# One level of Strassen for the up projection of a ConvFFN, with a separate down projection and buffers placed by lifetimes

## The chip, the cores and the metric

The kernel runs on one core of a Trainium2 chip. A core has TensorE (matrix products into PSUM, "PE" in the profile; its weight loads are "PEld"), VectorE ("DVE"), ScalarE ("ACT"), GpSimd ("POOL") and SyncE ("SP"), whose queue issues all of this kernel's DMAs. The metric is the device time of one execution in microseconds, as the median of several runs.

## The reference, cut to what matters

One layer (`DEPTH = 1`) of a backbone over 2048 latent tokens and 128 context tokens, `D_MODEL = 1024`, `D_FF = 2816`, all in float32: adaLN-modulated norm, a bidirectional HGRN2 mixer with eight heads, gated residual; then adaLN-modulated norm, a ConvFFN, gated residual; final norm.

```python
def conv_ffn(h, w_up, conv_w, conv_b, w_down, grid_axis):
    a, g = jnp.split(h @ w_up, 2, axis=-1)
    a = token_conv(a, conv_w, conv_b, grid_axis)
    return (jax.nn.silu(a) * g) @ w_down
...
hp = modulate(xp, norm_ffn_w[l], mod_p[3], mod_p[4])
hs = modulate(xs, norm_ffn_w[l], mod_s[3], mod_s[4])
xp = xp + mod_p[5] * conv_ffn(hp, ffn_w_up[l], ffn_conv_w[l], ffn_conv_b[l], ffn_w_down[l], None)
xs = xs + mod_s[5] * conv_ffn(hs, ffn_w_up[l], ffn_conv_w[l], ffn_conv_b[l], ffn_w_down[l], 2)
y_prompt = rms_norm(xp, final_norm_w)
y_sample = rms_norm(xs, final_norm_w)
```

`token_conv` is a convolution of width 3 along the tokens of a grid row (64 tokens) for the latent tokens, along the whole sequence for the context.

## The kernel before

Features lie on partitions, tokens along the free axis. The 2176 tokens are five pieces: four of 512 latent tokens (p = 0 to 3) and the context with 128 (`CTX`, p = 4). Each float32 product is made of three float16 products (`mm3`, L301 to L304): both factors are split into a high and a low float16 part, and high x high, high x low and low x high add up in PSUM. All matmuls of the projections are recorded under L302, L303 and L304, so a profile tells them apart by their tiles.

The stages follow each other: adaLN and norm 1 (0 to about 60 us), eight heads of HGRN2 (each has projections for all pieces, between which the scan's small products are set), the output projection with norm 2 (`project`, L841; `norm2`, L867), and the ConvFFN from about 1395 us on.

The ConvFFN runs eleven rounds `c2`, each over two blocks of 128 channels of the 22. A round loads six weight tiles (`ffn_weights`, L880: a and g of the up projection for two blocks, and two blocks of w_down), which `load_w` (L291) casts to a high part on ACT (L296) and a low part on DVE (L299). For each piece and block, `up` (L940) makes 24 products for a and 24 for g, 512 columns wide, with eight blocks of K; then the convolution on ACT and DVE (L952 to L958), SiLU (L960), the product with g (L961) and the split of u (L963, L964). `down` (L967) of the piece before comes between the two blocks' `up`: eight output blocks m, each six products over the round's two blocks of u, which DVE adds to the residual in SBUF (L974). The last round splits piece 3 into two halves of 256 tokens and starts the final norms (`final_norm`, L921) between its pieces; L931 (DVE) and L933/L934 (ACT and POOL) scale the outputs in turn.

A norm is a generator: `begin` runs its first step (squares on ACT, L246 and L249, sums on DVE, L250), and each later `tick` one more: the sum over features on TensorE (L254), the power on POOL (L230), a diagonal (L232), its spread over the partitions on TensorE (L240), and the modulation (`modulated`, L272: L277 and L286 on DVE, L281 on ACT).

SBUF tiles come from one pool in which every tag has a number of slots (`BUFS`, L81): eight of 4 KB for weights (`wp`), two for their raw form (`wr`), 32 for `H`, which hold first the normed inputs and later the residuals. A tile waits for the release of its slot. PSUM has two tags of four banks each: `pj` for projections, `sc` for the rest. The waits between engines are put in by the framework. The instructions of one engine are not strictly in the order of the text: on ACT, the weight casts of the next round (L296) run between steps of `up` (L952, L960) that the text has earlier.

## Time and profile before

| what | value |
|---|---|
| median of 3 runs | 2891.61 us (2889.58 to 2893.44) |
| span of the profiled execution | 2890.3 us |
| TensorE busy | 2847.3 us, 99% of the span |
| VectorE busy | 1747.1 us, 60% |
| ScalarE busy | 830.9 us, 29% |
| mean granted TensorE clock | 0.995 |
| one round of the ConvFFN | 132.7 us |

Of the profiled execution the profile gives the span, from its first to its last instruction; the three times are of other executions. A busy TensorE says little alone: its products overlap in the records (a product of 512 columns is recorded with 0.38 us, while the next starts 0.22 us after it), so the distance of the starts is what counts. A row of a group of instructions reads: line, engine, operation, output <- inputs, shapes, count, then the busy time in us and the mean ns of one, then the idle time before them and what ended it.

### The profile page before, as it was taken

To read this page: it belongs to the slowest core of one execution; us is meant where nothing else is said; L and a number is where in the kernel's file an instruction comes from. 1 tells how busy PE (TensorE), PEld (TensorE's weight loads), DVE (VectorE), ACT (ScalarE), POOL (GpSimd) and SP (SyncE) were. 2 spreads that over 40 slices of the span, in tenths; PEclk is the share of its full clock that TensorE was granted. 3 is DMA by queue.
4 is the path that set the end of the run, shared out by engine and by line. 5 is a ranking of instruction groups with operands and counts; after the bars stand their busy time and mean duration, and the time that the engine had idled before them with its cause. 6 is when DMAs were issued, how large, how long until landed. Compare 5 with 4: busy or idle time off the path is not lost.

```text
span 2890.3 us, 46289 instructions
## 1 busy us (share of the span) xinstructions
PE 2847.3 (99%) x18968; PEld 1675.7 (58%) x18968; DVE 1747.1 (60%) x4854; ACT 830.9 (29%) x1761; POOL 91.9 (3%) x101
## 2 busy tenths in 40 slices
PE   8999999999999999999999999999999999999996
PEld 4677777777777777655544445454545444454555
DVE  7978787878776767757564444343434444443457
ACT  5533333333433333324231112121212111111233
POOL 0100000000000000000000000000000000000013
PEclk9999999999999999999999999999999999999998
DMA  7011202020201020431101000010101010010002
GB/s 275 19 61 33 83 30 86 28 88 28 88 11 47 11 63 17 169 106 31 43 7 38 16 29 30 15 44 1 44 1 44 2 43 15 30 30 15 15 30 95
DMA packets 60867, 134.67 MB, mean 47 GB/s; under 512 B 8560, under 2 KB 18928, under 8 KB 60656
## 3 DMA queue, kind: packets, MB, share of 16 engines
q1 hardware_dynamic: 60656, 131.73, 14.1%
q8 instruction: 148, 2.42, 0.3%
q14 instruction: 63, 0.52, 0.1%
HBM read 112.83 MB, written 18.87 MB: 46 GB/s over the span
## 4 chain that ended last, share of the span: by engine, by line
PE 84%; DVE 10%; issue 1%; ACT 1%; DMA 1%; POOL 1%; POOLq 0%; DVEq 0%; ACTq 0%
PE pj L304 18%; PE pj L303 18%; PE pj L302 18%; PE sc L302 5%; PE sc L304 5%; PE sc L303 5%; PE pj L426 3%; PE pj L425 3%; PE pj L424 3%; PE sc L578 2%; PE sc L538 1%; PE sc L547 1%; DVE og L212 1%; PE sc L616 1%; PE sc L613 1%
## 5 line engine op out<-in xcount | busy, mean ns | idle before, releaser
L304 PEld LDWEIGHTS <-wp 128*128 128x128 f16 x3968 | 388.6, 98 | 368.0 <-issue 3.7
L302 PEld LDWEIGHTS <-wp 128*128 128x128 f16 x3968 | 389.7, 98 | 358.1 <-issue 5.6
L303 PEld LDWEIGHTS <-wp 128*128 128x128 f16 x3968 | 388.9, 98 | 358.8 <-issue 7.5
L974 DVE SCALAR_TENSOR_TENSOR H<-sc,g,H 128x512 f32<-128x512 f32 (+1 forms) x360 | 263.8, 738 | 137.3 <-PE sc L304 137.3
L302 PE MATMUL pj<-H,wp 128*128 128x512 f16 x880 | 334.7, 381 | 3.3 <-ACT H L281 3.3
L303 PE MATMUL pj<-H,wp 128*128 128x512 f16 x880 | 334.9, 381 | 0.8 <-DVE H L286 0.6
L304 PE MATMUL pj<-H,wp 128*128 128x512 f16 x880 | 335.4, 381 | 0.0
L956 DVE SCALAR_TENSOR_TENSOR SB<-pj,cws,SB 128x504 f32<-128x504 f32 (+2 forms) x112 | 73.4, 655 | 349.5 <-ACT SB L952 349.5
L952 ACT ACTIVATE SB<-pj,pv,cws 128x512 f32<-128x512 f32 (+2 forms) x112 | 79.2, 707 | 703.1 <-PE pj L304 702.0
L425 PE MATMUL pj<-wp,H 128*128 128x256 f16 x1024 | 279.4, 273 | 0.6 <-DVE wp L299 0.6
L426 PE MATMUL pj<-wp,H 128*128 128x256 f16 x1024 | 279.4, 273 | 0.0
L424 PE MATMUL pj<-wp,H 128*128 128x256 f16 x1024 | 279.4, 273 | 0.0
L961 DVE SCALAR_TENSOR_TENSOR SB<-pj,SB 128x512 f32<-128x512 f32 (+2 forms) x112 | 67.5, 602 | 246.3 <-PE pj L304 243.7
L299 DVE SCALAR_TENSOR_TENSOR wp<-wr,wp 128x1024 f16<-128x1024 f32 x106 | 128.8, 1224 | 88.1 <-ACT wp L296 76.1
L296 ACT ACTIVATE wp<-wr 128x1024 f16<-128x1024 f32 x106 | 110.1, 1049 | 118.3 <-DMA wr<-w_in 74.1
L960 ACT ACTIVATE SB<-SB 128x512 f32<-128x512 f32 (+2 forms) x112 | 62.6, 559 | 162.7 <-DVE SB L958 162.6
L426 PEld LDWEIGHTS <-H 128*128 128x128 f16 x1024 | 100.2, 98 | 12.4 <-issue 0.7
L425 PEld LDWEIGHTS <-H 128*128 128x128 f16 x1024 | 100.2, 98 | 11.7
L424 PEld LDWEIGHTS <-H 128*128 128x128 f16 x1024 | 100.2, 98 | 11.3
L397 ACT ACTIVATE f<-pj 128x512 f32<-128x512 f32 x64 | 38.0, 596 | 174.7 <-PE pj L304 174.4
L304 PE MATMUL pj<-op,wp 128*128 128x512 f16 (+1 forms) x232 | 87.2, 376 | 0.0
L303 PE MATMUL pj<-op,wp 128*128 128x512 f16 (+1 forms) x232 | 87.2, 376 | 0.0
(357 smaller groups left out, 5928.0 us busy)
## 6 DMA issues: line engine op xcount, KB each, us to landing
wr<-w_up SPq DMA_DIRECT2D x44, 512.0 KB, 4.0
wr<-w_in SPq DMA_DIRECT2D x40, 512.0 KB, 4.0
wr<-adaT SPq DMA_DIRECT2D x32, 512.0 KB, 3.6
wr<-w_down SPq DMA_DIRECT2D x22, 512.0 KB, 3.8
sp<-oT SPq DMA_DIRECT2D x32, 256.0 KB, 2.4
H<-xT SPq DMA_DIRECT2D x32, 256.0 KB, 4.6
yT<-H SPq DMA_DIRECT2D x24, 256.0 KB, 2.2
wr<-w_out SPq DMA_DIRECT2D x8, 512.0 KB, 4.2
```

The lines of the kernel that those rows point to most:

```text
L296: A.activation(dsthi, r3, AF.Copy, scale=scale)
L299: V.scalar_tensor_tensor(dstlo, r3, scale, dsthi, ALU.mult, ALU.subtract)
L302: T.matmul(out, whl[0], hhl[:, 0, :n], start=first, stop=False)
L303: T.matmul(out, whl[0], hhl[:, 1, :n], start=False, stop=False)
L304: T.matmul(out, whl[1], hhl[:, 0, :n], start=False, stop=last)
L424: T.matmul(o, hp[k][:, 0, tok], wvg[0][:, k], start=(k == 0), stop=False)
L425: T.matmul(o, hp[k][:, 0, tok], wvg[1][:, k], start=False, stop=False)
L426: T.matmul(o, hp[k][:, 1, tok], wvg[0][:, k], start=False, stop=(k == KT - 1))
L952: A.activation(y[:, :n], pa[:, :n], AF.Identity, bias=cbias, scale=w1)
L956: V.scalar_tensor_tensor(y3[:, :, 1:], a3[:, :, : row - 1], w0, y3[:, :, 1:], ALU.mult, ALU.add)
L961: V.scalar_tensor_tensor(y[:, :n], pg[:, :n], IWS, y[:, :n], ALU.mult, ALU.mult)
L974: V.scalar_tensor_tensor(x, pd[:, :n], g64[:, 1, m, s : s + 1], x, ALU.mult, ALU.add)
```

## The change

The kernel's text is built twice: once against stand-ins that count operations and note each tile's first and last use, then, with the addresses that `place` finds from these lifetimes, for the chip. There are no more slots: each tile has an address of its own for its lifetime, and what it must wait for is what used that address before. Tiles older than AGE operations take the first address that is free; younger ones the address that has been and stays free the longest. HGRN2 and what lies before it keep their operations.

The up projection takes blocks of two channel blocks (256 channels) by 1024 features by 512 tokens, and halves each of the three: w_up into A11 to A22, the normed input into B11 to B22. Seven products (`PROD`) of four K blocks and 256 columns take the place of eight, in the order 1, 2, 6, 5, 7, 3, 4, for a and g in turn. Three PSUM banks (A, B, C) hold running sums, which are read between products: each copy (ACT) and each addition (DVE) takes 256 columns into the four quarters c11 to c22 of an output tile in SBUF. `quad` makes the seven weight operands (A11, A12, A21, A22, S1 to S4) for a or g, each split in two parts; `operands` makes the seven input operands once for each piece, after the norm, in the place of the residual, which `keep` has written to DRAM before. The context's up projection keeps its products, with the weights A11 to A22.

After the products, `gate` does the convolution, SiLU and the product with g from SBUF; u is written to DRAM (`put_u`). Steps of `quad`, `gate` and `load_wd` wait in a list, `pending`, from which `post` takes one after each pair of products. When all 22 blocks are done, `down` runs over the pieces: for each of eight output blocks 66 products over all 22 channel blocks into one bank, one addition to the residual (read back from DRAM), and a final norm for each piece, with DVE alone scaling the outputs. w_down is loaded by output block (eight tiles of 22 blocks), during the last round of the up projection; u is read in 14 and 8 blocks for each piece.

```diff
--- before.py
+++ after.py
+def place(tiles, FAR, AGE):
+    at = [0] * len(tiles)
+    for grain, lo, hi, some in (
+            (TINY, 0, TINIES, [i for i, t in enumerate(tiles) if t.size <= 256]),
+            (GRAIN, TINIES, ARENA, [i for i, t in enumerate(tiles) if t.size > 256])):
+        slots = (hi - lo) // grain
+        lives = [[] for _ in range(slots)]
+        size = lambda i: -(-tiles[i].size // grain)
+        age = lambda i: tiles[i].last - tiles[i].born
+        some.sort(key=lambda i: (-age(i) // AGE if age(i) > AGE else 0, -min(size(i), 16),
+                                 tiles[i].born))
+        for i in some:
+            t, n = tiles[i], size(i)
+            packed = age(i) > AGE
+            room = []
+            for s in range(slots):
+                lv = lives[s]
+                j = bisect.bisect(lv, (t.born, 0))
+                before = t.born - lv[j - 1][1] + 1 if j else NEVER
+                after = lv[j][0] - t.last + 1 if j < len(lv) else NEVER
+                room.append(min(before, after))
+            step = 1 if n < 2 else 2 if n < 3 else 4
+            best, where = 0, -1
+            for st in (step, 1):
+                for s in range(0, slots - n + 1, st):
+                    g = min(FAR, *room[s : s + n])
+                    if g > best:
+                        best, where = NEVER if packed else g, s
+                if where >= 0:
+                    break
+            if where < 0:
+                return None
+            for s in range(where, where + n):
+                bisect.insort(lives[s], (t.born, t.last))
+            at[i] = lo + where * grain
+    return at
...
+    def keep(p):
+        n = PIECES[p][1]
+        xsp[p] = drt([P, KT, n], F32, f"xsp{p}")
+        for i in range(0, KT, 2):
+            nc.sync.dma_start(xsp[p][:, i : i + 2], X[p][:, i : i + 2])
+    def split(dst, src, scale=None):
+        A.activation(dst[0], src, AF.Copy)
+        V.tensor_tensor(dst[1], src, dst[0], ALU.subtract)
+    def operands(p, x):
+        TT[p] = {}
+        def half2(z, src):
+            t = TT[p][z] = tl([P, 2, 4, HN], F16, "T")
+            split((t[:, 0], t[:, 1]), src)
+        b11, b12, b21, b22 = (x[:, 4 * k : 4 * k + 4, HN * j : HN * j + HN]
+                              for k in range(2) for j in range(2))
+        half2("B11", b11)
+        half2("B21", b21)
+        yield
+        half2("B22", b22)
+        V.tensor_tensor(b11, b12, b11, ALU.subtract)
+        half2("T1", b11)
+        yield
+        V.tensor_tensor(b12, b22, b12, ALU.subtract)
+        half2("T3", b12)
+        V.tensor_tensor(b22, b22, b11, ALU.subtract)
+        half2("T2", b22)
+        yield
+        V.tensor_tensor(b21, b21, b22, ALU.subtract)
+        half2("T4", b21)
+    def norm2(p):
+        x = X[p]
+        n = PIECES[p][1]
+        s = int(p == CTX)
+        keep(p)
+        def finish(bc):
+            for k in range(KT):
+                V.scalar_tensor_tensor(x[:, k], x[:, k], wmod[:, 1, k, s : s + 1], bc[:, :n],
+                                       ALU.mult, ALU.mult)
+                A.activation(x[:, k], x[:, k], AF.Identity, bias=mod[:, 24 + k, s : s + 1])
+                if k == 3:
+                    yield
+            yield
+            if p == CTX:
+                TT[p] = tl([P, 2, KT, n], F16, "T")
+                split((TT[p][:, 0], TT[p][:, 1]), x)
+            else:
+                yield from operands(p, x)
+        def steps():
+            bc = []
+            yield from norm([x[:, k] for k in range(KT)], n, ["s", "s", "s"], "s", V, bc.append)
+            yield from finish(bc[0])
+        begin(steps())
...
+    def quad(cb, i):
+        w = {}
+        WQ[cb, i] = w
+        def part(z, src):
+            t = w[z] = tl([P, 2, 512], F16, "w7")
+            A.activation(t[:, 0], src, AF.Copy, scale=WS)
+            V.scalar_tensor_tensor(t[:, 1], src, WS, t[:, 0], ALU.mult, ALU.subtract)
+        raw = []
+        for j in range(2):
+            raw.append(tl([P, D], F32, "r"))
+            nc.sync.dma_start(raw[j], w_up[cb + j, i])
+        yield
+        a11, a12, a21, a22 = (raw[j][:, 512 * k : 512 * k + 512]
+                              for j in range(2) for k in range(2))
+        part("A11", a11)
+        part("A12", a12)
+        yield
+        s1, s2 = tl([P, 512], F32, "s"), tl([P, 512], F32, "s")
+        V.tensor_tensor(s1, a21, a22, ALU.add)
+        V.tensor_tensor(s2, s1, a11, ALU.subtract)
+        part("S2", s2)
+        yield
+        part("S1", s1)
+        s3 = tl([P, 512], F32, "s")
+        V.tensor_tensor(s3, a11, a21, ALU.subtract)
+        part("S3", s3)
+        yield
+        s4 = tl([P, 512], F32, "s")
+        V.tensor_tensor(s4, a12, s2, ALU.subtract)
+        part("S4", s4)
+        part("A22", a22)
+        part("A21", a21)
+    WQ = {}
+    PROD = {1: ("A11", "B11", "A", True), 2: ("A12", "B21", "B", True),
+            6: ("S2", "T2", "A", False), 5: ("S1", "T1", "C", True),
+            7: ("S3", "T3", "A", False), 3: ("S4", "B22", "C", False),
+            4: ("A22", "T4", "A", False)}
+    def product(q, i, w, T7):
+        za, zb, bank, first = PROD[i]
+        if first:
+            q[bank] = pt([P, 512], "pj" if bank == "A" else "sc")
+        out = q[bank][:, :HN]
+        wt, tt = w[za], T7[zb]
+        for k in range(4):
+            ks = slice(k * P, k * P + P)
+            for n, (a, b) in enumerate(((0, 0), (0, 1), (1, 0))):
+                T.matmul(out, wt[:, a, ks], tt[:, b, k], start=first and k == 0 and n == 0,
+                         stop=i in (2, 3, 4) and k == 3 and n == 2, skip_group_check=True)
+        sc = q["scale"]
+        (c11, c12), (c21, c22) = ([m[:, HN * j : HN * j + HN] for j in range(2)] for m in q["out"])
+        def add(dst, src):
+            V.scalar_tensor_tensor(dst, src, sc, dst, ALU.mult, ALU.add)
+        if i == 1:
+            A.activation(c11, out, AF.Copy, scale=sc)
+        elif i == 2:
+            add(c11, out)
+        elif i == 6:
+            A.activation(c12, out, AF.Copy, scale=sc)
+        elif i == 7:
+            A.activation(c22, out, AF.Copy, scale=sc)
+            add(c22, q["C"][:, :HN])
+        elif i == 3:
+            add(c12, out)
+        elif i == 4:
+            A.activation(c21, out, AF.Copy, scale=sc)
...
+    def put_u(y, cb, p, n):
+        u = tl([P, 2, 512], F16, "u")
+        split((u[:, 0, :n], u[:, 1, :n]), y[:, :n])
+        USP[cb, p] = drt([P, 2, n], F16, f"u{cb}_{p}")
+        nc.sync.dma_start(USP[cb, p], u[:, :, :n])
+    pending = []
+    def post(n=1):
+        for _ in range(n):
+            while pending and next(pending[0], 0) == 0:
+                pending.pop(0)
+    def gate(cb, p, qa, qg):
+        for j in range(2):
+            y = conv(qa["out"][j], cb + j, p, 512)
+            yield
+            V.tensor_tensor(y, y, qg["out"][j], ALU.mult)
+            put_u(y, cb + j, p, 512)
+            yield
+    def up(cb, p):
+        qa, qg = ({"scale": s, "out": [tl([P, 512], F32, "c7") for _ in range(2)]}
+                  for s in (1.0, IWS))
+        for i in (1, 2, 6, 5, 7, 3, 4):
+            product(qa, i, WQ[cb, 0], TT[p])
+            product(qg, i, WQ[cb, 1], TT[p])
+            post()
+            tick()
+        pending.append(gate(cb, p, qa, qg))
+    def up_ctx(cb):
+        n = NCTX
+        for j in range(2):
+            pa, pg = pt([P, 512], "pj"), pt([P, 512], "pj")
+            for pp, i in ((pa, 0), (pg, 1)):
+                for k in range(KT):
+                    wt = WQ[cb, i][("A11", "A12", "A21", "A22")[2 * j + k // 4]]
+                    ks = slice(k % 4 * P, k % 4 * P + P)
+                    mm3(pp[:, :n], (wt[:, 0, ks], wt[:, 1, ks]), TT[CTX][:, :, k], n,
+                        k == 0, k == KT - 1)
+            y = conv(pa[:, :n], cb + j, CTX, n)
+            V.scalar_tensor_tensor(y[:, :n], pg[:, :n], IWS, y[:, :n], ALU.mult, ALU.mult)
+            put_u(y, cb + j, CTX, n)
+            post()
+    WD = {}
+    U = {}
...
+    def load_wd(m):
+        w = tl([P, 2, NCB, P], F16, "wd")
+        WD[m] = w
+        for c0, c1 in ((0, 11), (11, 22)):
+            raw = tl([P, 11, P], F32, "rawd")
+            nc.sync.dma_start(raw, w_down[c0:c1, :, m * P : (m + 1) * P]
+                              .rearrange("k p c -> p k c"))
+            A.activation(w[:, 0, c0:c1], raw, AF.Copy, scale=WS)
+            V.scalar_tensor_tensor(w[:, 1, c0:c1], raw, WS, w[:, 0, c0:c1],
+                                   ALU.mult, ALU.subtract)
+            yield
+    def load_u(p, cbs):
+        n = PIECES[p][1]
+        for cb in cbs:
+            u = tl([P, 2, n], F16, "U")
+            nc.sync.dma_start(u, USP[cb, p])
+            U[p, cb] = u
+    XD = {}
+    def down(p, m, c, n):
+        s = int(p == CTX)
+        x = tl([P, n], F32, "x")
+        nc.sync.dma_start(x, xsp[p][:, m, c : c + n])
+        pd = pt([P, 512], "pj")
+        for cb in range(NCB):
+            mm3(pd[:, :n], (WD[m][:, 0, cb], WD[m][:, 1, cb]), U[p, cb][:, :, c : c + n], n,
+                cb == 0, cb == NCB - 1)
+        V.scalar_tensor_tensor(x, pd[:, :n], g64[:, 1, m, s : s + 1], x, ALU.mult, ALU.add)
+        XD.setdefault((p, c), []).append(x)
...
+    pending.extend([quad(0, 0), quad(0, 1)])
     for m in range(KT):
         project(3, ALL, (m,))
         project(CTX, ALL, (m,))
         tick()
         if m == 1:
             norm2(2)
+        if m > 1:
+            post(2)
+    post(20)
+    norm2(3)
+    norm2(CTX)
+    for cb in range(0, NCB, 2):
+        last = cb + 2 == NCB
+        for p in range(CTX):
+            up(cb, p)
+            if p == 1 and cb:
+                up_ctx(cb)
+            if not last and p in (1, 2):
+                pending.append(quad(cb + 2, p - 1))
+            if last:
+                pending.extend([load_wd(2 * p), load_wd(2 * p + 1)])
+                if p == 2:
+                    load_u(0, range(14))
+        if cb == 0:
+            up_ctx(cb)
+    post(100)
+    load_u(0, range(14, NCB))
+    for p in range(CTX + 1):
+        n = PIECES[p][1]
+        for m in range(KT):
+            down(p, m, 0, n)
+            tick()
+            if m == 3 and p < CTX:
+                load_u(p + 1, range(14))
+        if p < CTX:
+            load_u(p + 1, range(14, NCB))
+        final_norm(p, 0, n, [V])
     while norms:
         tick()
```

364 lines of the change are left out of this document (159 added, 205 removed), and 5 rows, old and new, of the table BUFS.

## The prediction

> **What bounds the kernel now.** I read the page first, then the shapes on TensorE, then tables by stage.
>
> ```profile
> span 2890.3 us, 46289 instructions
> PE 2847.3 (99%) x18968; PEld 1675.7 (58%) x18968; DVE 1747.1 (60%) x4854; ACT 830.9 (29%) x1761; POOL 91.9 (3%) x101
> PE 84%; DVE 10%; issue 1%; ACT 1%; DMA 1%; POOL 1%; POOLq 0%; DVEq 0%; ACTq 0%
> ...
> 434.70:579.50 144.80, 144.14 (x1209) 104.02 (x1207) 116.97 (x449) 51.71 (x137) 5.28 (x5) 1.00 0.19 58
> 868.50:1012.50 144.00, 144.00 (x1209) 103.97 (x1207) 98.96 (x417) 51.90 (x137) 5.06 (x5) 1.00 0.09 29
> ...
> 1296.00:1399.00 103.00, 102.10 (x638) 54.92 (x637) 73.75 (x113) 38.74 (x55) 3.03 (x3) 1.00 0.16 49
> 1399.00:1477.00 78.00, 78.00 (x372) 36.61 (x371) 46.24 (x73) 23.09 (x39) 1.55 (x2) 1.00 0.02 7
> 1531.70:1664.40 132.70, 132.54 (x722) 64.43 (x721) 57.51 (x86) 24.07 (x37) 0.00 (x0) 1.00 0.08 24
> ```
>
> The last rows are stages (start:end, length, then busy time of PE, PEld, DVE, ACT, POOL; granted clock; DMA share; GB/s): two heads of HGRN2, the output projection, the first 78 us of the ConvFFN, one ConvFFN round of two channel blocks. TensorE is busy without a hole in each, at a granted clock of 1.00. Busy time alone doesn't prove saturation, since products overlap; the starts do:
>
> ```profile
> 1899.69 0.38 PE L303 MATMUL pj<-V,wp 128*128 128x512 f16 x1
> ...
> 1908.54 0.22 PE L302 MATMUL pj<-q,wp 128*128 128x128 f16 x1
> ...
> 2808.75 0.27 PE L302 MATMUL pj<-k,wp 128*128 128x256 f16 x1
> ...
> 2813.99 0.38 PE L302 MATMUL sc<-o,wp 128*128 128x512 f16 x1
> ...
> 1911.22 0.38 PE L302 MATMUL sc<-o,wp 128*128 128x512 f16 x1
> ...
> L304 PEld LDWEIGHTS <-wp 128*128 128x128 f16 x3968 | 388.6, 98 | 368.0 <-issue 3.7
> ```
>
> From 1899.69 to 1908.54 start 41 products of 512 columns: 0.2159 us each. From there to 1911.22 start 48 of 128 columns: 0.0558 each. From 2808.75 to 2813.99 start 48 of 256 columns (the last round halves piece 3): 0.1092 each. So columns set the time, and a 256-column product costs 0.506 of a 512-column one, its weight load (98 ns in the last row) hidden. A round holds 4 x 144 products of 512 and 144 of 128: 124.4 + 8.0 = 132.4 us, against 132.7 in the row. The stage is saturated: only less TensorE work, or idle time outside it, can shorten the kernel.
>
> **The change, term by term.**
>
> *Up products.* Before, a round takes 4 pieces x 96 products of 512 columns; over 11 rounds 4224 x 0.2159 = 912.0 us. After, each piece takes 7 block products x 12 x 2 (a and g) = 168 of 256 columns: 7392 x 0.1092 = 807.2 us. **Saved: 104.8 us.** Context up products and all down products keep their numbers and widths (528 x 4 of 512 columns); down only sums over 22 blocks in PSUM instead of 2.
>
> The Trainium skill, "TensorE: Matmul & The Clock Gate", section "Back-to-back issue gap", also gives a gap of N/2.4 + 2.5 ns; it says too that a stream of load and product pairs holds about 81 ns at N=128 and 131 ns at N=512. By the second rule the new products would cost at least 7392 x 81 ns = 599 us against 553 us before, a loss; the trace (55.8 and 215.9 ns) contradicts it.
>
> *Vector and scalar work beside the up products.*
>
> ```profile
> L974 DVE SCALAR_TENSOR_TENSOR H<-sc,g,H 128x512 f32<-128x512 f32 x344 | 256.4, 750 | 137.3 <-PE sc L304 137.3
> L974 DVE SCALAR_TENSOR_TENSOR H<-sc,g,H 128x256 f32<-128x256 f32 x16 | 7.4, 478 | 0.0
> L956 DVE SCALAR_TENSOR_TENSOR SB<-pj,cws,SB 128x504 f32<-128x504 f32 x86 | 63.9, 743 | 338.1 <-ACT SB L952 338.1
> L964 DVE TENSOR_TENSOR og<-SB,og 128x512 f16<-128x512 f32 x22 | 15.2, 692 | 13.6 <-ACT og L963 13.6
> L299 DVE SCALAR_TENSOR_TENSOR wp<-wr,wp 128x1024 f16<-128x1024 f32 x106 | 128.8, 1224 | 88.1 <-ACT wp L296 76.1 <-PE pj L304 11.2
> L952 ACT ACTIVATE SB<-pj,pv,cws 128x512 f32<-128x512 f32 x86 | 66.9, 778 | 601.3 <-PE pj L304 600.2 <-DVE og L250 0.6 <-DVE Am L286 0.5
> L960 ACT ACTIVATE SB<-SB 128x512 f32<-128x512 f32 x86 | 54.1, 630 | 142.7 <-DVE SB L958 142.7
> L618 ACT ACTIVATE op<-sc 128x256 f32<-128x256 f32 x64 | 23.8, 372 | 19.1 <-PE sc L616 19.1
> ```
>
> Columns: busy us, mean ns of one, then idle before. Per piece: six Strassen additions out of PSUM at 0.48 = 2.9 us on DVE and eight copies at 0.37 = 3.0 on ACT; the gate twice, each (2 x 0.743 + 2 x 0.692) = 2.9 on DVE and (0.778 + 2 x 0.63) = 2.0 on ACT. Per round two `quad`s, each seven parts at 0.75 plus four sums at 0.69 = 8.0 us DVE and seven casts at 0.63 = 4.4 ACT. A round: DVE 4 x 8.7 + 16 + 2.5 (context) = 53 us, ACT 4 x 7 + 8.8 + 2.2 = 39, against 4 x 168 x 0.1092 + 5.4 = 78.8 us of TensorE. Both fit under it. What is new is a tight hand-off: bank C is read (ACT copy of product 7, then DVE addition) before product 3 may write it. From the last start of 7a: 0.27 + 0.37 + 0.48 us plus hand-overs is about 1.2; TensorE has the 12 products of 7g in between, 13 x 0.1092 = 1.4 us. It just fits if both engines are free. The two HGRN2 rows show what crowded engines cost: DVE at 117 instead of 99 us of 144 cost 0.8 us, 0.6%. Bounds: 0 (hidden) to 12 us a round (the slower rival). I take 1.4 us a round, near that row with a little for the round's edge, where `quad` of g comes late: **+15 us.** A wait there holds the products behind it, and nothing else.
>
> *The entry of the ConvFFN.* Norm 2 of a piece had 16 DVE operations of 0.75 (12 us); now it has 8, seven splits and four differences of 1024 elements. The nearest rows give 1.22 to 2 x 0.69, so 6 + 11 x 1.33 = 20.6: 8.7 us more. The 1296:1399 row leaves 29 us free on DVE; three norms add about 24 and quads instead of six weight casts (7.3) add 8.7, so DVE is over full, 4 us behind. Then piece 3 needs its norm (7 additions, 20.6: 26 us), the context 6, four pieces' additions 12 and three gates 17, together 61, within the 55 us of three pieces that hide it, 10 us behind; a second round of quads, 16, follows in the same queue. **+18 us**, bounds 0 (gates put off) and 35 (all overhang paid, chain latency too).
>
> *Tail.*
>
> ```profile
> 2826.00:2866.00 40.00, 35.51 (x367) 31.41 (x365) 33.93 (x62) 16.84 (x42) 14.34 (x10) 1.00 0.28 106
> 2866.00:2891.00 25.00, 7.04 (x48) 5.92 (x47) 14.99 (x37) 3.61 (x12) 7.74 (x10) 0.55 0.32 105
> ...
> 2870.03 1.01 PE L254 MATMUL pj<-ones,kvb 128*128 128x1 f32 x4 [3.19 <-DVE kvb L250]
> 2880.86 0.28 DVE L250 TENSOR_TENSOR kvb<-kvb,qb 128x128 f32<-128x128 f32 x1
> ```
>
> TensorE's last product ends 3.2 us before 2870.03, at 2866.8; the last norms still run then, and 4.5 of the 40 us before are idle. After, norms of pieces 0 to 2 lie beside the next piece's 114 us of down products, that of piece 3 beside the context's 29 us, and only the context's is left: from the last sum (2880.86) to the end 9.4 us, plus about 1.1 for the last update and square. 23.5 - 10.5 + 4.5, about **-18 us**, bounds -22 and -8.
>
> *Turn from up to down.* Before it is nothing: both alternate. Now 8 weight blocks (11.5 MB) and piece 0's u (5.8 MB) have to be there.
>
> ```profile
> 1180.00:1200.00 20.00, 19.41 (x207) 15.70 (x204) 7.95 (x20) 8.51 (x18) 0.00 (x0) 1.00 0.94 341
> wr<-w_down SPq DMA_DIRECT2D x22, 512.0 KB, 3.8
> ```
>
> 17.3 MB at 341 GB/s are 51 us, inside the last round's 79. Their SP issues share the queue with 10 stores of u; a load queued behind the last gate's store waits for it. The first 14 blocks of u are 42 products, 9 us of cover. **+5 us**, bounds 0 and 30. Storing u (24.5 MB) and reading it again, and x, is hidden at a DMA share of 0.08.
>
> *Buffers.*
>
> ```profile
> 22.37 1.06 ACT L296 ACTIVATE wp<-wr 128x1024 f16<-128x1024 f32 x1 [3.99 <-DMA wr<-w_in]
> ```
>
> HGRN2 at 144 us a head is at its products' floor, so there is little to gain; at the start weights come late through the two slots of `wr` (4 us here). **-2 us**, bounds -8 and +8 (an address reused too soon makes a DMA wait, and SP's queue behind it).
>
> Sum: 2890.3 - 104.8 + 15 + 18 - 18 + 5 - 2 = 2803.5. Medians stand 1.3 us above this span (2891.6 against 2890.3): **2805 us**.
>
> **Rivals.**
>
> *All hidden* (20%). DVE's 53 of 79 us leaves room; entry, hand-offs and turn at nothing or nearly (4 us): 2891.6 - 104.8 - 18 - 8 + 4 = 2765. Against it: DVE's overhang at the entry is counted work.
>
> *DVE and ACT become the bound of the up stage: slower* (12%). A gate's half is one chain over both: 0.78 + 1.49 + 0.63 + 0.69 + 0.63 + 0.69 = 4.9 us. Were both queues bound to the program's order, nothing would run beside it, and a piece with a quad beside it would take 9.8 + 5.9 (copies, additions) + 8.6 = 24.3 us instead of 18.3; two such pieces a round lose 12 us, 132 in all: 2805 - 15 + 132 = 2922. It decides from a loss of 9 us a round on. Against it:
>
> ```profile
> 1910.09 0.46 ACT L952 ACTIVATE SB<-pj,pv,cws 128x128 f32<-128x128 f32 x1
> 1910.44 1.04 ACT L296 ACTIVATE wp<-wr 128x1024 f16<-128x1024 f32 x1
> 1911.64 0.31 ACT L960 ACTIVATE SB<-SB 128x128 f32<-128x128 f32 x1 [0.15 <-DVE SB L958]
> ```
>
> The weights of the next round (L296), written later in the program, run between two steps of one context block (L952, L960): the queues are filled by readiness.
>
> *Addresses and DMAs* (14%). w_down now comes in 512-byte pieces, and long-lived tiles take the first address free, even one just read. If the turn costs 30 us and each of four later pieces 2: 2805 - 5 + 38 = 2838.
>
> *Narrow products cost more than half* (1%). A weight load of 98 ns that isn't hidden would make 7392 x 0.207 = 1530 us of the up products, and 3510 in all; the 48 starts above speak against it. The second rule of the Trainium skill's page above is of this kind, milder: 46 us lost by its figures.
>
> **How the numbers follow.** Forecast 2805 has 53%. The range, 2762 to 2860, takes in the hidden case and the addresses, and leaves out the slower rival and some of its milder forms. A measurement here tells about 0.2% (6 us) from no change. Faster: forecast, hidden and addresses less small tails, 0.84; within 0.2%: 0.03; slower: 0.13.
>
> **What would show it.** Right: TensorE starts at 0.109 us throughout up; a round of up near 80 us; holes in TensorE in 1300 to 1480 released by DVE; one short norm behind the last product. Wrong: holes before product 3 or 7 in every round released by ACT or DVE (slower rival); at the turn, TensorE released by DMAs of u or w_down (addresses); heads longer than 144.8 us.

## The result, and the profile after

| | before | after |
|---|---|---|
| median of 4 runs | 2892.23 us (2889.58 to 2893.44) | 2792.88 us (2789.91 to 2796.14) |
| ratio | | 0.9656, 95% interval 0.9642 to 0.967 |
| span of the profiled execution | 2890.3 us | 2788.1 us |

The change makes the kernel 3.4% faster, 102.2 us by the two spans. The first lines and the chain of the page of the changed kernel:

```profile
span 2788.1 us, 53502 instructions
PE 2745.6 (98%) x21992; PEld 1974.3 (71%) x21992; DVE 1709.5 (61%) x4924; ACT 1007.6 (36%) x2233; POOL 68.3 (2%) x80
...
PE 88%; DVE 7%; DMA 2%; ACT 1%; issue 1%; SPq 0%; POOL 0%; POOLq 0%; DVEq 0%; ACTq 0%
```

TensorE is still the bound, with 3024 more and narrower products. To see where time is lost, cut the ConvFFN at the products that open its stages. In the timeline of TensorE (start, length, engine, line, operation) these are the first up product, the first context product of round 0, that of the last round, and the first down product:

```profile
1397.29 0.38 PE L1060 MATMUL pj_p<-T,w 128*128 128x256 f16 x2
...
1480.54 0.22 PE L394 MATMUL pj_p<-T,w 128*128 128x128 f16 x1
...
2232.76 0.22 PE L394 MATMUL pj_p<-T,w 128*128 128x128 f16 x1
...
2285.54 0.38 PE L394 MATMUL pj_p<-U,wd 128*128 128x512 f16 x1
```

The table of windows between such cuts (length, then busy time of PE, PEld, DVE, ACT, POOL; granted clock; DMA share; GB/s):

```profile
1397.30:1480.50 83.20, 77.90 (x695) 68.40 (x693) 72.48 (x123) 48.57 (x92) 2.02 (x2) 0.98 0.16 53
1480.50:1522.60 42.10, 42.10 (x435) 38.28 (x434) 21.43 (x42) 18.65 (x40) 0.00 (x0) 1.00 0.18 58
1522.60:1601.30 78.70, 78.70 (x770) 71.06 (x768) 47.61 (x88) 37.36 (x79) 0.00 (x0) 1.00 0.17 57
2073.80:2152.50 78.70, 78.70 (x770) 71.10 (x769) 47.46 (x88) 37.11 (x79) 0.00 (x0) 1.00 0.17 56
2152.50:2232.80 80.30, 79.13 (x771) 71.16 (x770) 51.14 (x89) 39.81 (x80) 0.00 (x0) 1.00 0.44 129
2232.80:2285.50 52.70, 45.76 (x434) 39.73 (x432) 32.46 (x47) 27.95 (x46) 0.00 (x0) 0.94 0.78 236
2285.50:2778.00 492.50, 492.45 (x2706) 243.59 (x2704) 82.30 (x124) 31.46 (x53) 4.04 (x4) 1.00 0.22 73
2778.00:2788.10 10.10, 1.15 (x4) 0.80 (x4) 3.27 (x12) 0.59 (x2) 0.55 (x1) 0.64 0.18 52
```

The third and fourth rows are whole rounds, context product to context product: 4 x 168 x 0.1092 + 96 x 0.0558 = 78.74 us of starts, and 78.7 is what they take. The steady rounds lose nothing; VectorE works 48 of the 79 us. The losses lie at both ends. Four pieces take 73.4 us of starts in the first row, which lasts 83.2. The sixth row, two pieces and a context block, should take 42.05 and takes 52.8; the fifth loses 1.5 more. The down projection (seventh row) has no hole, and behind its last product (2778.0) come 10.1 us. Before, 16.7 us came behind the last product of the down projection, the context's, which ended at 2873.6; in the timeline of before:

```profile
2873.31 0.31 PE L304 MATMUL sc<-sg,wp 128*128 128x128 f16 x1
```

A wait of 3.2 us and the norms' sums stood ahead of the last 24 of these products, which then ran at a granted clock of 0.50 (2870.9 to 2873.6 us). In the changed kernel, the waits of TensorE name who releases it (total us, times, longest):

```profile
PE sc_p L1060 <- DVE c L1066: 8.4, 4, 3.7
...
PE pj_p L1060 <- ACT c L1069: 2.4, 2, 1.6
...
PE pj_p L1060 <- ACT c L1075: 1.8, 1, 1.8
```

All are hand-offs of PSUM banks: L1069 and L1075 copy a bank on ScalarE, L1066 adds one on VectorE. The largest, at the end of the last round, in the timelines of ScalarE, VectorE and TensorE:

```profile
2252.04 1.38 ACT L1158 ACTIVATE wd<-rawd 128x1408 f16<-128x1408 f32 x1 [2.80 <-DMA rawd<-w_down]
2253.32 0.64 ACT L1075 ACTIVATE c<-pj_p 128x256 f32<-128x256 f32 x2
...
2253.45 1.62 DVE L1159 SCALAR_TENSOR_TENSOR wd<-rawd,wd 128x1408 f16<-128x1408 f32 x1 [2.23 <-ACT wd L1158]
2254.99 0.75 DVE L1066 SCALAR_TENSOR_TENSOR c<-sc_p,c 128x256 f32<-128x256 f32 x2
...
2255.46 0.80 PE L1060 MATMUL sc_p<-T,w 128*128 128x256 f16 x3 [3.67 <-DVE c L1066]
```

Read it upwards from the last row. TensorE waits for the addition at 2254.99. That stands on VectorE behind the low-part cast of w_down, which waits for the high-part cast on ScalarE, which waits for a DMA; the copies of the bank (2253.32) stand behind the same cast. So a late DMA stops TensorE through two queues, although TensorE needs nothing of w_down yet. The copies and additions themselves take about 0.4 us each. The DMA engines were busy throughout: the windows below show a DMA share of 1.05 to 1.09 from 2252 to 2258 us. After such a wait the granted clock drops; windows of 2 us over the same place:

```profile
2252.00:2254.00 2.00, 0.00 (x0) 0.00 (x0) 0.55 (x1) 1.92 (x3) 0.00 (x0) 1.00 1.05 384
2254.00:2256.00 2.00, 0.54 (x3) 0.40 (x3) 1.74 (x3) 0.00 (x0) 0.00 (x0) 0.78 1.08 367
2256.00:2258.00 2.00, 2.00 (x12) 1.35 (x10) 0.00 (x0) 0.00 (x0) 0.00 (x0) 0.50 1.09 272
2258.00:2260.00 2.00, 2.00 (x17) 1.69 (x16) 0.84 (x2) 0.99 (x2) 0.00 (x0) 0.86 0.07 19
```

The two waits 2277.24 (1.79 us) and 2278.97 (1.24 us) have the same chain. With 0.25 at 2249.01 they make 7.0 us; the dips of the clock behind them take the rest of the stage's 10.7.

Last, the first up product came at 1394.47 us before and comes at 1397.29 now, 2.8 us later. In the timeline of before, then of after, with one wait of the HGRN2 stage that before does not have:

```profile
1394.47 0.38 PE L302 MATMUL pj<-op,wp 128*128 128x512 f16 x1
```

```profile
150.41 0.56 PE L346 MATMUL sc_p<-ones,og 128*128 128x1 f32 x2 [3.60 <-DVE k L593]
```

The sum over the context's features waits 3.6 us for VectorE, which does scan work first.

### The profile page after: what moved, and what is told of

Same layout as the page of the kernel before. It is cut to its first block, busy times and chain, and to the rows that moved or that the text cites. A ratio compares the mean times of both kernels' runs of the same rounds, so it can differ in the third digit from the quotient of the medians.

```text
span 2788.1 us, 53502 instructions
## 1 busy us (share of the span) xinstructions
PE 2745.6 (98%) x21992; PEld 1974.3 (71%) x21992; DVE 1709.5 (61%) x4924; ACT 1007.6 (36%) x2233; POOL 68.3 (2%) x80
## 4 chain that ended last, share of the span: by engine, by line
PE 88%; DVE 7%; DMA 2%; ACT 1%; issue 1%; SPq 0%; POOL 0%; POOLq 0%; DVEq 0%; ACTq 0%
PE pj_p L1060 15%; PE pj_p L396 13%; PE pj_p L395 13%; PE pj_p L394 13%; PE sc_p L1060 12%; PE pj_p L518 4%; PE pj_p L516 4%; PE pj_p L517 4%; PE sc_p L670 2%; PE sc_p L630 1%; PE sc_p L639 1%; PE sc_p L705 1%; PE sc_p L775 1%; DVE T L949 1%; PE sc_p L708 1%; DVE X L984 1%
## 5 line engine op out<-in xcount | busy, mean ns | idle before, releaser
L1060 PEld LDWEIGHTS <-w 128*128 128x128 f16 x7392 | 724.9, 98 | 100.7 <-issue 14.7
L1060 PE MATMUL pj_p<-T,w 128*128 128x256 f16 x4224 | 485.8, 273 | 4.5 <-ACT c L1069 2.4
L1060 PE MATMUL sc_p<-T,w 128*128 128x256 f16 x3168 | 371.6, 274 | 8.4 <-DVE c L1066 8.4
L395 PE MATMUL pj_p<-U,wd 128*128 128x512 f16 (+1 forms) x880 | 296.5, 347 | 0.0
L394 PE MATMUL pj_p<-U,wd 128*128 128x512 f16 (+1 forms) x880 | 296.5, 347 | 0.0
L396 PE MATMUL pj_p<-U,wd 128*128 128x512 f16 (+1 forms) x880 | 296.4, 347 | 0.0
L396 PE MATMUL pj_p<-H,wp 128*128 128x512 f16 x768 | 292.0, 380 | 1.0 <-DVE wp L391 1.0
L394 PE MATMUL pj_p<-H,wp 128*128 128x512 f16 x768 | 290.6, 379 | 2.4 <-ACT H L373 2.0
L395 PE MATMUL pj_p<-H,wp 128*128 128x512 f16 x768 | 292.1, 380 | 0.0
L516 PE MATMUL pj_p<-wp,H 128*128 128x256 f16 x1024 | 279.4, 273 | 0.4 <-ACT wp L388 0.4
L518 PE MATMUL pj_p<-wp,H 128*128 128x256 f16 x1024 | 279.4, 273 | 0.0
L517 PE MATMUL pj_p<-wp,H 128*128 128x256 f16 x1024 | 279.3, 273 | 0.0
L1066 DVE SCALAR_TENSOR_TENSOR c<-sc_p,c 128x256 f32<-128x256 f32 x264 | 109.2, 421 | 203.5 <-ACT c L1075 183.5
L396 PEld LDWEIGHTS <-wp 128*128 128x128 f16 x960 | 94.2, 98 | 91.2 <-DVE wp L391 1.1
L394 PEld LDWEIGHTS <-wp 128*128 128x128 f16 x960 | 94.2, 98 | 83.6 <-issue 3.9
L395 PEld LDWEIGHTS <-wp 128*128 128x128 f16 x960 | 94.1, 98 | 81.1 <-issue 1.6
L396 PEld LDWEIGHTS <-wd 128*128 128x128 f16 x880 | 86.1, 98 | 83.1
L394 PEld LDWEIGHTS <-wd 128*128 128x128 f16 x880 | 86.4, 98 | 82.3
L395 PEld LDWEIGHTS <-wd 128*128 128x128 f16 x880 | 86.1, 98 | 82.4
L394 PE MATMUL pj_p<-og,wo 128*128 128x512 f16 (+1 forms) x320 | 107.9, 347 | 1.4 <-DMA og<-sp 1.3
```

The source lines that it names most:

```text
L394: T.matmul(out, whl[0], hhl[:, 0, :n], start=first, stop=False)
L395: T.matmul(out, whl[0], hhl[:, 1, :n], start=False, stop=False)
L396: T.matmul(out, whl[1], hhl[:, 0, :n], start=False, stop=last)
L516: T.matmul(o, hp[k][:, 0, tok], wvg[0][:, k], start=(k == 0), stop=False)
L517: T.matmul(o, hp[k][:, 0, tok], wvg[1][:, k], start=False, stop=False)
L518: T.matmul(o, hp[k][:, 1, tok], wvg[0][:, k], start=False, stop=(k == KT - 1))
```

## The experiments

All run beside the kernel before on the same chip, so ratios to before are compared; the changed kernel's is 0.9656 (0.9642 to 0.967).

### Strassen alone undone

```diff
-        for i in (1, 2, 6, 5, 7, 3, 4):
-            product(qa, i, WQ[cb, 0], TT[p])
-            product(qg, i, WQ[cb, 1], TT[p])
+        for j in range(2):
+            pa, pg = pt([P, 512], "pj"), pt([P, 512], "pj")
+            for pp, i in ((pa, 0), (pg, 1)):
+                for k in range(KT):
...
+                    mm3(pp, (wt[:, 0, ks], wt[:, 1, ks]), TT[p][:, :, k], 512,
+                        k == 0, k == KT - 1)
```

> The changed kernel with Strassen alone undone: the up projection is 8 plain block products a round again (4224 products of 512 columns), the four quarters A11..A22 are only cast and the operand is only split; the separate down projection, the trip of its input through DRAM and the placement by lifetimes stay. Theory (the products carry the gain, the other terms cancel): the products come back at +104.8 us, the differences of the operands at the entry go (about -7 us), so 2792.9 + 98 = 2891 us, 2880 to 2898. Rival (the separate down projection and its shorter tail carry a good part of the gain): about 2850 us.

Measured: 2876.56 us, ratio 0.994 (0.9924 to 0.9955); between the theory and its rival. Its windows, up stage and the rest:

```profile
1399.20:2372.00 972.80, 972.80 (x5305) 474.56 (x5302) 361.44 (x558) 274.53 (x444) 1.52 (x2) 1.00 0.21 66
2372.00:2874.80 502.80, 493.38 (x2709) 244.14 (x2707) 82.95 (x131) 30.63 (x50) 4.58 (x5) 1.00 0.20 67
```

TensorE is busy throughout its up stage. Against the changed kernel's 888.2 us (1397.3 to 2285.5) Strassen brings 84.6 us, not 104.8: 20.2 come back as losses inside the stage. And without Strassen the kernel is 16.7 us under before: the separate down projection and its short tail carry that, less what the buffers cost. So the terms don't cancel as the theory had it. This kernel also casts w_down in its last round, from the same DMAs, and TensorE never waits: a bank takes 24 products of 512 columns (5.2 us) and is written again three banks later, which leaves some 15 us for its evacuation. Strassen's hand-offs leave 1.3.

### The placement alone

```diff
-        return sb.tile(shape, dt, tag=tag, name=f"{tag}_{uid[0]}", bufs=bufs)
+        return nc.alloc_sbuf_tensor_at(f"{tag}_{uid[0]}", shape, dt,
+                                       offset=base + at[uid[0] - 1])[:]
```

> The kernel before with one part of the change alone: its buffers placed by lifetimes, as in the changed kernel, instead of pools. Theory: the first up product came 2.6 us later in the changed kernel than before, with 6.2 us lost at 140 to 160 us behind the context's norm and 3.6 won back at the transitions of the heads, and the placement is the cause of all of it: +0.1%, about 2895 us (2888 to 2898), with the loss at 140 to 160 us in its trace too. Rival (the loss at 140 to 160 us comes from something else, such as the changed order of the later program): no such loss, 2886 to 2892 us.

Measured: 2897.45 us, ratio 1.0015 (1.0006 to 1.0023), +4.2 us by the medians. The wait is there too, in the timeline of TensorE:

```profile
153.39 0.56 PE L346 MATMUL sc_p<-ones,og 128*128 128x1 f32 x2 [3.60 <-DVE k L593]
```

So this wait belongs to the placement. With other release times of buffers, it seems, work comes to VectorE in another order; which buffer does it was not traced. It also differs from kernel to kernel: in the runs of this study that leave all work before the ConvFFN alone, the first up product comes between 1396.7 and 1402.5 us.

### The hand-offs of the banks

Three kernels. Two add VectorE work behind each pair of products but the first (two operations, as here, or four):

```diff
+            for _ in range(2 if i > 1 else 0):
+                c11 = qa["out"][0][:, :HN]
+                V.tensor_tensor(tl([P, HN], F32, "junk"), c11, c11, ALU.mult)
             post()
```

> The changed kernel with added work: after each pair of narrow products but the first of an up projection, VectorE multiplies a 256-wide part of a result with itself twice more (0.42 us each; the results are not used), about 20 us a round on the 48 us of VectorE in a round of 78.7 us. Theory (in the steady rounds the hand-offs of the PSUM banks are hidden, because VectorE and ScalarE have slack behind each pair of products, 11 us of PE): the rounds stay under 79.5 us and the time grows by no more than 6 us, 2790 to 2799 us. Rival (the additions are near their due time, so that more work ahead of them shows at once): every round grows by several us, 2820 us or more.

> As the run with two added VectorE operations, with four of them after each pair of products: about 40 us a round more, so that VectorE has 88 us of work in a round whose products take 78.7 us. Theory: here VectorE becomes the bound, a round takes at least 88 us and the time grows by 90 us or more, to 2880 to 2930 us. Rival (some of the additions merge or the counted 48 us is too high): 2800 to 2850 us.

Measured: 2809.12 us, ratio 0.971 (0.9695 to 0.9724), and 2860.69 us, ratio 0.9892 (0.9877 to 0.9906). Rounds of 80.2 to 81.2 and of 85.4 to 87.9 us. One window of each, first with two, then with four:

```profile
1700.00:1780.00 80.00, 77.92 (x760) 70.09 (x759) 62.52 (x134) 36.92 (x77) 0.00 (x0) 1.00 0.16 55
```

```profile
1700.00:1780.00 80.00, 75.15 (x713) 66.33 (x712) 72.33 (x167) 36.27 (x76) 0.00 (x0) 0.98 0.15 52
```

Both theories missed, in opposite ways. The added operations overlap in the queue and cost 0.32 us each, so two make VectorE 63 us of an 81 us round, not 68. Already this shows: 2.2 us a round, by waits for the additions L1066 (16 between 1530 and 2150 us, up to 1.7 us). With four it is busy for 90% of the time and a round loses about 7.5 us. VectorE as the bound thus doesn't set in at a point: at 61% of a round nothing was lost, at 78% 2.2 us, at 90% 7.5. (The expectations give a pair of products 11 us of TensorE; it is 24 x 0.1092 = 2.6 us.) But even 30 us more of VectorE in every round leave the kernel under before.

The third takes the seven products of a first, then those of g:

```diff
-        for i in (1, 2, 6, 5, 7, 3, 4):
-            product(qa, i, WQ[cb, 0], TT[p])
-            product(qg, i, WQ[cb, 1], TT[p])
+        for n, (q, w, i) in enumerate((q, w, i) for q, w in ((qa, 0), (qg, 1))
+                                      for i in (1, 2, 6, 5, 7, 3, 4)):
+            product(q, i, WQ[cb, w], TT[p])
...
```

> The changed kernel with the order of the products changed: the seven products of a run first and then the seven of g, instead of a pair of a and g of each number. The products, copies and additions are the same. What separates two products of one bank falls from a product of the other half (1.3 us of PE) to the next product of the same half. Theory (the interleaving is the cover of the hand-offs of the banks): each re-use of a bank now waits for the copy or the addition of 0.36 to 0.42 us and what stands ahead of it, 1.2 to 2.4 us in each of the 44 up projections, 2845 to 2900 us. Rival (the copies would be ready in time anyway): 2790 to 2800 us.

Measured: 2820.09 us, ratio 0.9745 (0.9729 to 0.9761). A round takes 81.8 to 83.0 us, on average 3.7 more: 0.93 us for each up projection, 27 us in all. That is less than the theory's 1.2 to 2.4 us and its 2845 us, and more than the rival's nothing. So the interleaving of a and g is the cover that the steady rounds live on, at a lower price than expected.

### The entry of the ConvFFN

One kernel leaves the four differences of `operands` out, the other makes them on GpSimd; the edit of the first of the four, in the second kernel:

```diff
-        V.tensor_tensor(b11, b12, b11, ALU.subtract)
+        G.tensor_tensor(b11, b12, b11, ALU.subtract)
```

> The changed kernel without the four differences of the operand's quarters for each piece (sixteen subtractions of VectorE, 1024 elements a lane, 1.21 us each; the quarters are split as they are, and the products are made of those). Theory (the entry loses 6.8 us because VectorE is busy without a break there, and the differences, 19 us, are what overhangs): the entry from the first up product to the first context product takes under 79 us (83.2 with them), the time is 4 to 7 us shorter, 2786 to 2789 us. Rival (the casts of the weights and the additions hold the first products up in any case): 82 us or more, 2791 to 2794 us.

> The changed kernel with the same sixteen subtractions on GpSimd instead of VectorE. No duration of a subtraction of this size on GpSimd stands in these traces, so this run measures it. Theory (VectorE's overhang is the entry's loss, and GpSimd has 2% of the span in use): as without them, 4 to 7 us shorter, 2786 to 2789 us. Rival (GpSimd takes several times VectorE's 1.21 us, so that the splits behind the differences are late, or it slows VectorE while it runs): no gain or a loss, 2792 to 2805 us.

Without the differences: 2793.0 us, ratio 0.9657 (0.9644 to 0.967). The entry takes 81.7 us instead of 83.2; 19 us of VectorE work bring 1.5. The theory falls: the amount of VectorE work at the entry is not what costs. (The total doesn't show even these 1.5, because the last round lost 7 us more than in the changed kernel, with other addresses.) Kernels that keep all the differences do better: with a before g the entry takes 78.9 us, and in the five kernels of the next section, whose entry has the changed kernel's text and other addresses, 80.0 to 82.3 us.

The changed kernel's trace shows what its largest wait at the entry hangs on. In the timelines of ScalarE, VectorE and TensorE:

```profile
1451.55 0.63 ACT L1013 ACTIVATE w<-s 128x512 f16<-128x512 f32 x1 [3.33 <-DMA u<-u]
...
1454.08 0.37 ACT L1075 ACTIVATE c<-pj_p 128x256 f32<-128x256 f32 x1
...
1454.81 0.42 DVE L1066 SCALAR_TENSOR_TENSOR c<-sc_p,c 128x256 f32<-128x256 f32 x1
...
1455.29 4.25 PE L1060 MATMUL sc_p<-T,w 128*128 128x256 f16 x24 [2.36 <-DVE c L1066]
```

A cast of the next round's weights waits 3.3 us for the DMA that stores a u; two steps of a gate, the copy and the addition come behind it. It is the chain of the last round, with a store in the place of a read. With the low clock behind it (24 products in 4.05 us instead of 2.62) this wait costs 3.8 of the entry's 7.7 us. In the kernel that spreads the loads of u (next section) such casts wait 0.4 us, TensorE waits 0.7 for this addition, and the entry takes 80.1 us. That the cast waits because its tile takes over the address of u is likely, but was not tried apart. An earlier wait (1.59 us at 1401.89, for a copy behind two casts on ScalarE) does hang on the differences, as each of the casts waits for one of them.

With the differences on GpSimd: 2824.32 us, ratio 0.976 (0.9747 to 0.9773), 31 us slower than with them on VectorE, and beyond the rival's 2805. Of the 28.5 us between the two spans, 16.5 come before the first up product and 11.1 in the entry. In the timelines of VectorE and GpSimd:

```profile
1397.02 6.20 DVE L1014 SCALAR_TENSOR_TENSOR w<-s,w 128x512 f16<-128x512 f32 x3
...
1414.47 5.46 DVE L342 TENSOR_TENSOR s<-s,s 128x512 f32<-128x512 f32 x3
...
1397.18 2.73 POOL L965 TENSOR_TENSOR X<-X 128x1024 f32<-128x1024 f32 x1 [17.53 <-DVE T L949]
1399.99 2.68 POOL L968 TENSOR_TENSOR X<-X 128x1024 f32<-128x1024 f32 x1
1414.68 2.67 POOL L970 TENSOR_TENSOR X<-X 128x1024 f32<-128x1024 f32 x1 [12.02 <-DVE T L949]
1417.43 2.34 POOL L973 TENSOR_TENSOR X<-X 128x1024 f32<-128x1024 f32 x1
```

Three casts that take about 2 us elsewhere take 6.2, and three sums that take 1.3 take 5.5, at about the time in which GpSimd subtracts. Moving the work gives VectorE nothing, and GpSimd takes 2.3 to 3.2 us where VectorE took 1.21.

### The last round

Five kernels. First, w_down read for one block only, all casts kept:

```diff
-            raw = tl([P, 11, P], F32, "rawd")
-            nc.sync.dma_start(raw, w_down[c0:c1, :, m * P : (m + 1) * P]
+            if m == 0:
+                RAW.append(tl([P, 11, P], F32, "rawd"))
+                nc.sync.dma_start(RAW[-1], w_down[c0:c1, :, m * P : (m + 1) * P]
...
+            raw = RAW[c0 // 11]
```

> The changed kernel, but each of the two halves of w_down's raw tile is read from DRAM for the first block of rows alone, and the casts of the other seven blocks take that tile again (most of the reading of w_down is left out, the casts are all there). Theory (in the last round casts stand in the queues of ScalarE and VectorE, wait for late DMAs, and hold up the evacuations behind them): the PE's waits in the last round fall from 8.1 us to under 3, and with the clock that comes back the time falls 8 to 12 us, to 2781 to 2785 us. Rival (it is the casts' own 1.4 and 1.6 us that make the evacuations late): the waits and the time stay, 2790 to 2795 us.

Second, all read, the DMA of each half at least one step ahead of its casts:

```diff
+        fetch(0, 11)
+        yield
+        fetch(11, 22)
+        cast(raws[0], 0, 11)
+        yield
+        cast(raws[1], 11, 22)
```

> The changed kernel with the reading of w_down put ahead of its casts: the DMA of a block's first half is issued as soon as the block is due, that of the second half one step (a pair of narrow products, 11 us of PE) ahead of its casts; the same DMAs and casts otherwise. Theory (late DMAs under the casts): waits of the last round under 3 us, the time 6 to 12 us shorter, 2781 to 2787 us. Rival (the casts' own length, or the DMA queue that the loads of u fill, whatever the order): 2790 to 2795 us.

Third, the loads of u spread as well; fourth, these on a queue of their own (the last two lines):

```diff
-                if p == 2:
-                    load_u(0, range(14))
...
+            if cb + 2 == NCB and p == 3 and len(U) < NCB - 2:
+                load_u(0, range(len(U), min(len(U) + 4, NCB)))
...
-            nc.sync.dma_start(u, USP[cb, p])
+            (nc.sync if p else nc.gpsimd).dma_start(u, USP[cb, p])
```

> The changed kernel with w_down's DMAs ahead of their casts as in the run before, and the loads of u for the first down products spread over the last up projection, four after each of its pairs of products, instead of fourteen at once behind the third. Theory (what is left of the waits in the last round, 7.9 us, comes from casts that wait for DMAs behind that burst: DMA at 290 to 350 GB/s at 2270 to 2274 us): the waits of the last round fall under 3 us, the first down product comes at most 45 us after the last context product (48.9 with the burst), and the time is 2780 to 2785 us. Rival (the casts' own 1.4 and 1.6 us ahead of the evacuations): the waits stay at 6 us or more and the time at 2786 to 2790 us.

> The changed kernel with w_down's DMAs ahead of their casts and the loads of u spread, as in the run before, and with the loads of u for the first piece issued from GpSimd's queue instead of SyncE's. Theory (with the loads spread, a load of u that waits for its room stood in SyncE's queue ahead of w_down's DMAs, SyncE's waits of up to 9.4 us on PE, and the casts then waited for those): the casts wait for DMA under 4 us in all (13.1 in that run), the waits of PE in the last round fall under 3 us, 2781 to 2785 us. Rival (the casts' own length decides, or a DMA of 0.7 MB takes 5 to 8 us whatever stands ahead): no change from that run, 2786 to 2790 us.

Fifth, from the second: only two of the eight blocks of w_down are cast in the last round.

```diff
+                if p < 2:
+                    pending.append(load_wd(p))
+                    next(pending[-1])
...
+            if p == 0 and m + 2 < KT:
+                for _ in load_wd(m + 2):
+                    pass
             down(p, m, 0, n)
```

> The changed kernel with the casts of w_down taken out of the last round of up projections: only the blocks of rows 0 and 1 are read and cast there (beside the first and the second up projection, the reading one step ahead of the casts), blocks 2 to 7 beside the first six blocks of the down projection of the first piece, two blocks (28 us) ahead of their use. All DMAs, casts and products are the same, and the loads of u stand where the change has them. Theory (what the last round loses comes from the casts of w_down that stand, waiting for DMA, ahead of the evacuations, whatever queue carries the loads): the waits of PE in the last round fall under 2 us, its last context product to the first down product takes under 43.5 us (52.8 in the changed kernel, 42.1 without any loss), nothing is lost in the down projection, and the time falls 9 to 13 us, to 2779 to 2784 us. Rival (the loss only moves: the down projection then waits for w_down, or its additions stand behind the casts): 2786 to 2793 us.

Measured ("turn" is from the last round's context product to the first down product, without loss 42.05 us; waits are TensorE's in the last round; DMA is what the casts of w_down waited for their reads from 2150 to 2300 us):

| kernel | turn, us | waits, us | DMA, us | median, us | ratio |
|---|---|---|---|---|---|
| changed kernel | 52.8 | 8.0 | 14.5 | 2792.88 | 0.9656 (0.9642 to 0.967) |
| w_down read once | 45.4 | 4.5 | 2.6 | 2782.92 | 0.9617 (0.9604 to 0.963) |
| reads ahead | 48.9 | 7.9 | 13.7 | 2788.32 | 0.9637 (0.9624 to 0.965) |
| u spread | 47.9 | 6.6 | 13.1 | 2787.62 | 0.9637 (0.9623 to 0.9652) |
| u on GpSimd's queue | 51.4 | 9.2 | 20.5 | 2794.72 | 0.9659 (0.9646 to 0.9672) |
| casts in down | 49.4 | 4.2 | 10.1 | 2784.96 | 0.9626 (0.9613 to 0.9639) |

Every edit also moves addresses, and that, it seems, is enough to move this table. The kernel without the differences loads and casts w_down by the changed kernel's text, yet its casts wait 15.7 us for reads, TensorE waits 12.2 and the turn takes 55.2; with the differences on GpSimd the turn takes 53.6, with a before g 50.4. Against this spread only the first of the five stands clear; the others show a tendency at most.

The kernel that reads w_down once speaks for the main cause: with the casts all there and their data at hand, 7.4 of the turn's 10.7 us go, so most of the loss is not the casts' own length (the waits that stay, 4.5 us, are above the 3 that the theory allowed). But it also takes 10 MB of traffic from the DMA engines (share 0.54 in its turn, 0.78 in the changed kernel's); reads issued late and reads that are slow on busy engines are not told apart. The waits left over, in its list for the last round, are of the same hand-offs:

```profile
PE sc_p L1060 <- DVE c L1066: 2.4, 2, 1.5
PE pj_p L1060 <- ACT c L1075: 2.1, 1, 2.1
```

Reading one step ahead was too little: a step is one pair of products, 2.6 us of TensorE, and not the 11 us that the expectation gives. The casts still waited 13.7 us, and spreading the loads of u changed which cast waits, not that one does. In that kernel, ScalarE, VectorE, TensorE:

```profile
2226.30 1.38 ACT L1164 ACTIVATE wd<-rawd 128x1408 f16<-128x1408 f32 x1 [4.10 <-DMA rawd<-w_down]
...
2227.71 1.63 DVE L1165 SCALAR_TENSOR_TENSOR wd<-rawd,wd 128x1408 f16<-128x1408 f32 x1 [5.48 <-ACT wd L1164]
...
2229.72 1.47 PE L1060 MATMUL sc_p<-T,w 128*128 128x256 f16 x12 [2.70 <-DVE c L1066]
```

The reads take 4.5 to 8.6 us from issue to landing there. The loads of u ahead of them in SyncE's queue were not the obstacle: with u on another queue, the casts waited longer (20.5 us). In that kernel the DMA share was 1.06 to 1.14 from 2244 to 2260 us, around its longest waits, so a load on another queue met busy engines all the same. Why a read is issued as late as it is, by SyncE's order or by its room in SBUF, was not separated. The theories of these three kernels failed: none brought TensorE's waits under 3 us. With u spread the rival's numbers came out, but the kernel that reads w_down once speaks against its reason, the casts' own length.

The last kernel is the fastest that leaves nothing out, and its interval lies just below the changed kernel's; the profiled executions stand 4.2 us apart, the medians 7.9. The round before its turn takes 78.9 us (80.3 in the changed kernel), but the turn takes 49.4 us where the theory said under 43.5, because one wait of 4.0 us is left, again from ScalarE and TensorE:

```profile
2270.53 2.64 ACT L1162 ACTIVATE wd<-rawd 128x1408 f16<-128x1408 f32 x2 [5.86 <-DMA U<-u]
2273.08 0.64 ACT L1075 ACTIVATE c<-pj_p 128x256 f32<-128x256 f32 x2
...
2273.49 1.22 PE L1060 MATMUL pj_p<-T,w 128*128 128x256 f16 x5 [4.00 <-ACT c L1075]
```

Up to this copy ScalarE has done eight of these casts, though the program's text has four ahead of it:

```profile
L1162 ACT ACTIVATE wd<-rawd 128x1408 f16<-128x1408 f32 x8 | 10.9, 1371 | 10.9 <-DMA U<-u 5.9 <-DMA rawd<-w_down 5.0
```

The order of an engine is not that of the text; what sets it was not traced. Casts written later were put ahead of the copy, and then waited for a DMA, by the profile a load of u. The mechanism, a cast that waits for a DMA ahead of a copy, is the theory's; taking the casts out of the text's last round did not take all of them out of its queue.

## Why the prediction was right, term by term

Forecast 2805, measured 2792.88. By spans, the sum predicted -86.8 and -102.2 came out. That it came so near is in part luck: two terms were 25 us too dear together and two others 12 us too cheap. The terms, with the up stage's loss of 20.2 us split by its windows (the entry against 73.4 us of up products and 2.1 of the norms' sums):

| term | predicted | measured | by |
|---|---|---|---|
| up products | -104.8 | -104.8 | rounds of 78.7 us, half round of 42.0 |
| hand-offs beside up | +15 | 0 | the same rounds |
| entry of the ConvFFN | +18 | +7.7 | 83.2 us against 75.5 |
| last round and turn | +5 | +12.2 | 1.5 and 10.7 |
| down and tail | -18 | -20.2 | ConvFFN of the kernel without Strassen (1475.6 us) against before (1495.8) |
| buffers | -2 | +2.8 | first up product |

**Up products.** Right. Each product of 256 columns costs 0.1092 us, as the starts of before said, and nothing of the weight loads shows.

**Hand-offs.** The step that missed most. Its own count, 1.2 us of chain against 1.4 us of cover, was right, and the 15 us were put on top for a crowded engine, by the HGRN2 row (whose 0.8 us in 144 would be 0.4 in a round, not the 1.4 taken). But at 48 of 79 us VectorE wasn't crowded. The added-work kernels give the price that row stood for: 2.2 us a round at 63 us, 7.5 at 78.

**Entry.** Right sign, mis-sized: the working turned VectorE's overhang into delay one to one. Taking 19 us of that work away brought 1.5, and half of what was lost, 3.8 us, is one wait behind a cast that stood for a DMA.

**Turn.** Within its bounds, for a reason that the prediction didn't have. It looked for TensorE waiting at the turn for w_down or u; the down projection started without a wait. The DMAs were late to casts, and the casts held up the last up projections.

**Tail.** Right in mechanism and nearly in size, by one line misread: TensorE's last product did not end at 2866.8. The context's last 24 came behind the wait, up to 2873.6, so 1.3 of the 23.5 us (24 x 0.0558) are products. That leaves 22.2 us of loss before against 10.1 now, 12.1 less, and 4.5 of holes gone: 16.6. The other 3.6 us were not traced.

**Buffers.** Wrong in sign, within its bounds. Waits like the 3.6 us at 150 us, where a norm stands behind the scan, were not thought of.

**Rivals.** "All hidden" (2765) failed by the two ends of the up stage, 19.9 us, and by the 8 us that it gave the buffers. "DVE and ACT become the bound" failed by 30 us of VectorE a round: even the kernel with four added operations loses 7.5 us a round, under the 9 from which it decides. "Addresses and DMAs" had the right suspects, late DMAs and addresses, at a third of its price.

## What to carry to other kernels

When a change replaces loose hand-offs by tight ones (a bank read and rewritten within 1.3 us), look not at the engines' shares but at the longest instruction, and above all the longest wait, that can stand ahead of the evacuation in its queue; work that waits for a DMA doesn't belong there. It should be read further ahead than a read takes (here up to 8.7 us), or cast where nothing tight follows; neither was reached here. Where a framework orders the instructions, moving text is not enough: see in the trace where they landed. And price two parts of one change apart: here the up products brought 84.6 of their 104.8 us, and the separate down projection with its tail about 20.

## What the runs showed of the hardware

The granted clock falls to half after waits that are short beside this span. After a wait of 3.67 us it was 0.50 from 2256 to 2258 us and back at 1.00 by 2260. One of 2.36 us at the entry did it too:

```profile
1454.00:1456.00 2.00, 0.71 (x7) 0.64 (x7) 2.00 (x5) 1.97 (x6) 0.00 (x0) 1.00 0.35 49
1456.00:1458.00 2.00, 2.00 (x13) 1.43 (x12) 2.00 (x5) 0.76 (x2) 0.00 (x0) 0.60 0.87 290
1458.00:1460.00 2.00, 2.00 (x12) 1.40 (x10) 1.32 (x4) 1.47 (x3) 0.00 (x0) 0.54 0.14 54
1460.00:1462.00 2.00, 2.00 (x21) 1.79 (x20) 1.85 (x4) 1.10 (x3) 0.00 (x0) 1.00 0.30 41
```

Three to four microseconds at half rate add some 1.5 to 2 us to the wait. The waits of 1.7 us and less in the kernel with two added operations left it at 1.00. The Trainium skill's page "TensorE: Matmul & The Clock Gate", section "What's actually happening", says that the clock halves after an idle window of about 3.4 us; the drop agrees, but here 2.36 us of recorded wait were enough.

GpSimd's subtractions held up VectorE's operations on SBUF for most of their length: beside two of them (5.4 us) three casts took 6.2 us instead of 2, beside two more (5.0 us) three sums 5.5 instead of 1.3. The Trainium skill's "GPSIMD Engine Reference", section "Specifications", says that the two share their SBUF interfaces, with contention for VectorE instructions that have two SBUF inputs; both groups are of that kind.
